# A two-layer streaming encoder step: the main product stream of layer 0 shifted against its chain, and three small changes of order beside it

## The chip, the cores and the metric

The kernel runs on one core of one Trainium2 chip, as one program. The time is the device time of one execution in microseconds (us); the value of a kernel is the median of its runs. The profile is that of a single execution, recorded by the hardware profiler. The core's engines are TensorE (matmul, PE in the profile, with its weight loads as PEld), VectorE (DVE), ScalarE (ACT), GpSimd (POOL), and SyncE (SP), whose queue here issues nearly all DMAs.

## What is computed

The reference is one inference step of two layers over 512 prompt tokens and 32 sample tokens, width 1024. Layer 0 mixes tokens with RWKV-7, layer 1 with differential attention; both also attend to 256 memory rows in 4 heads and gate the result. Only layer 0 is touched by the change:

```python
def rwkv_layer(x, mk, mv, prev_row, S0, norm_w, w_out, w_in, mu, ...):
    h = rmsnorm(x, norm_w)
    p, qm, gate = jnp.split(h @ w_in, [RW_PROJ, RW_PROJ + MEM_W], axis=-1)
    y_mix, S_T, last_row = rwkv_mixer(p, prev_row, S0, mu, w0, w_up, a0, a_up, k_k, k_a, r_k, ln_w, ln_b)
    y_mem = mem_attention(qm, mk, mv)
    out = jnp.concatenate([y_mix.astype(x.dtype), y_mem], axis=-1) * jax.nn.silu(gate)
    return x + out @ w_out, S_T, last_row

# in rwkv_mixer, for each of 24 heads, token by token (S is 64 x 64):
def step(S, inp):
    r_t, k_t, v_t, w_t, kk_t, a_t = inp
    sa = jnp.einsum('bhvk,bhk->bhv', S, -kk_t)
    S = (S * w_t[:, :, None, :] + sa[..., None] * (kk_t * a_t)[:, :, None, :]
         + v_t[..., None] * k_t[:, :, None, :])
    return S, jnp.einsum('bhvk,bhk->bhv', S, r_t)

# mem_attention, per head: softmax(q k^T / sqrt(128)) v over 256 memory rows
```

The sample tokens start from a state that is given (`state_rwkv`), the prompt from zero.

## The kernel before

**Heads, pairs, chunks.** The 24 heads are worked in 12 pairs (two heads of 64 fill the 128 partitions). Within a pair the 512 prompt tokens are 8 chunks of 64, and the state goes from chunk to chunk: this is the *chain* (`rw_chain`, `chunk`). A chunk takes three steps. TensorE multiplies the state `SB` with the prepared operand `zr`, and VectorE adds the result into `avz`; TensorE multiplies `avz` with `at`, and ScalarE copies the result into `sv` and `yt` and scales the old state into `sd`; TensorE multiplies `sv` with `bt`, and VectorE makes the new state from it. The first chunk lacks the first step, so a pair has 23 chain steps. Each begins with a TensorE instruction that must wait for VectorE or ScalarE.

**The main stream.** The large projection `h @ w_in` (and the memory values) is cut into blocks of 128 output columns. A block is 48 matmuls of 128x272, here called main products: two token halves, eight slices of the inner dimension, and three products each, since every fp32 operand is split into a high and a low part (`whi`, `wlo` of the weights, `hh`, `hl` of the activations). `stream` (L1535) is a generator that gives the products of all blocks one at a time, so that they can be laid between the chain steps; in the trace they write the tile `ps_g`. At the head of a block it asks for weights two blocks ahead (`load`, two DMAs of 256 KB on SP's queue into `raw`) and puts the split of the next block's weights (ScalarE makes `whi`, VectorE `wlo`) on a list. At the end of a half block the result is evacuated: for a shift block, ScalarE copies it to `raw`, and a scaling (ScalarE) and an addition (VectorE, the tile is called `rkv`) are put on the same list; for a gate block, a tanh and a multiplication (`sg`).

**The put-off list.** `some` (L313) is called once per half step. It takes at most one VectorE item and one ScalarE item off the head of the list, a VectorE item only if an allowance permits. The allowance is `room` times the half steps so far, less what VectorE has been given already (`spent`), by the estimates in the plan. `until` empties the list up to an item when a reader needs it.

**The plan.** Each engine executes its instructions in the order in which the program issues them, and that order is written out by hand here. `PLAN` (L48) has one entry for each of the 23 steps of a pair, with two halves. Each names pieces of other work: `prep` prepares a later pair, `inv`, `back`, `at` and `mrg` invert small triangular blocks on GpSimd by way of DRAM, `val`, `out` and `fin` finish outputs, `smp` is the sample's chunk (`rw_sample`), `rsq` a reciprocal root. The two numbers beside a piece are its estimated time on TensorE and on VectorE. In pairs 10 and 11 there is nothing left to prepare, and `MPLAN` (L77) lays the steps of the memory attention there (`mem_steps`, L1223), one entry per call: keys and values are fetched, then per group of two token tiles the scores, the softmax, the transposes and at last the product with the values. `scores` has VectorE take the row maximum (`mnm`), and ScalarE the exponentials (`mp`, with their row sums `mrs`), and `weighted` has VectorE scale them. The PSUM pool of most of these small products, `psm`, has two buffers (L2160).

**How many products per step.** `each[pr]` is the number of main products of a pair: 192 in most pairs (four blocks), 144 in pair 9, which has only three, and 130 left over in pair 0. In pair 9, `KEPT` = 24 of them stay behind for the end of the pair. `whole` sums the TensorE estimates of the pair and 0.126 us per product, `due` cuts it into 23 equal parts (in pair 0 by the estimated VectorE load), and each half step issues products until its due time is reached. The blocks in their order are: for pair p up to 8, the k block of pair p+3, the gate of pair p-1, the r block and the v block of pair p+3; then queries, gates, and the first blocks of the output projection.

**The sample's state.** `rw_sample` (L983) fetches the pair's given state by two DMAs into `SS`, at its first call (step 4), transposes it there (`ps_si`), and goes through the chunk at the later `smp` entries.

Of the kernel before, what the change touches and what calls it, by code (L numbers as in the profile page):

```python
# [45 lines left out]
LATER = 0.75  # L46
FULL = ("full", 0, 0, 0)
PLAN = [  # L48
    [[("val", 0, 0.95, 0), ("prep", 2, 0.1, 0)], [("prep", 2, 0, 0.42)]],
    [[], [("prep", 2, 0, 1.04)]],  # L50
# [21 lines left out]
MEMPE = 4.8  # L72
SHIFTED, KEPT = 13, 24
LAM = 5
EARLY = 5
SPLIT = {10: (18,), 11: (1, 5, 9, 13)}
MPLAN = {10: [(0, 0), (2, 0), (3, 0), (4, 0), (5, 0), (6, 0), (6.5, 1), (7, 0), (8, 0), (9, 0), (10, 0), (11, 0), (11.5, 0), (12.5, 1),  # L77
# [3 lines left out]

# [26 lines left out]
class Trunk:  # L108
# [874 lines left out]
    def rw_sample(self, st):  # L983

        nc, p, pr = self.nc, self.rb2, st["pr"]
        sl = self.SS[pr % 2]
        for h in range(2):
            self.se.dma_start(sl[64 * h : 64 * h + 64, 64 * h : 64 * h + 64], self.a["state_rwkv"][0, 0, 2 * pr + h])
        yield
        ps = self.psm.tile([P, 4, P], F32, tag="m", name="ps_si")  # L990
        self.te.transpose(ps[:, 0, :], sl[:], self.ident[:])
        S = p.tile([P, P], F32, tag="ssi", name="ssi", bufs=1)
        self.ve.tensor_copy(S[:], ps[:, 0, :])
        yield from self.chunk(st, 8, S, sl)
        yield
        self.state_out(sl, self.o[8][0, 0, 2 * pr : 2 * pr + 2])
# [226 lines left out]
    def mem_steps(self, st, i, h, p, two):  # L1223
# [25 lines left out]
        def scores(tiles):  # L1249
# [9 lines left out]
            pt = p.tile([P, 2, NMEM], F32, tag="mp", name="mp", bufs=2)  # L1259
            self.ve.tensor_reduce(nm[:, :k], s, AX.X, ALU.max, negate=True)  # L1260
            for u in range(k):
                self.ae.activation(pt[:, u, :], s[:, u], AF.Exp, bias=nm[:, u : u + 1], accum_out=rs[:, u : u + 1])
# [18 lines left out]
        for t in groups[:2]:  # L1281
            yield
            scores(t)
            yield
            weighted()
# [5 lines left out]
        yield  # L1291
        scores(groups[2])
        yield
# [132 lines left out]
    def layer0(self, mem):  # L1426
# [6 lines left out]
        with ExitStack() as ctx:  # L1433
# [160 lines left out]
            for kind, n in zip(("mrg", "mrg", "val", "mrg"), FILL3):  # L1594
                go(kind, 0)
                fill(n)
            ready = len(FILL2) - 11
            each[0] -= sum(map(sum, (FILL0, FILL1, FILL2, FILL3))) - 4 * 24 - 6 * 48
            for pr in range(NPAIR):
# [3 lines left out]
                load = [HOPV[k % 3] + sum(us for x in y for kind, d, _, us in x if 0 <= pr + d < NPAIR) for k, y in enumerate(PLAN)]  # L1603
                whole = sum(took) + MEMPE * len(mplan) / 12 + MAIN * (each[pr] - kept)

                pace = [max(x, 1.4) for x in load] if each[pr] < 3 * 6 * KT else [1.0] * len(PLAN)
                due = [whole * sum(pace[:k]) / sum(pace) for k in range(len(PLAN) + 1)]
                room = (sum(load) + 2.3 * each[pr] / 48) / len(PLAN)
                t, left, spent = 0.0, each[pr] - kept, 0.0
                for k, y in enumerate(PLAN):  # L1610
# [3 lines left out]
                    for half, x in enumerate(y):  # L1614
# [7 lines left out]
                        for at, h in mplan:  # L1622
                            if at == k + half / 2:
                                if h not in mit:
                                    mit[h] = self.mem_steps(mems[h], 0, h, self.ma, 2)
                                    next(mit[h])
                                next(mit[h], None)
                                t += MEMPE / 12
                        if half and pr == LAM and k in (1, 7):
# [599 lines left out]
```

## Time and profile before

| | |
|---|---|
| runs | 1404.84 us median of 3 (1404.56 to 1409.58) |
| profiled execution | 1403.86 us, its span 1401.7 us |
| mean granted TensorE clock | 0.996 |
| layer 0, pairs 0 to 11 | 134.97 to 692.00 us of the span |
| HBM read and written | 111.12 MB and 22.91 MB |

The page's first part gives the busy time of each engine; its second part shows the span in 40 slices, where TensorE stands at 9 tenths or more in all slices but the first and the last. A matmul's end is modelled and reaches into the next one, so short pauses of TensorE do not show as idle time. The page's share of a line is of little use here, because one helper (L105) records every operation; the names of tiles tell the places apart. In the views, `a<-b,c` is a tile and what it was made from, and `[1.39 <-DVE avz]` is the idle time before an instruction and what ended it. In the lists of waits the three numbers are the total in us, the count, and the longest.

### The profile page before, as it was taken

To read this page: it belongs to the slowest core of one execution; us is meant where nothing else is said; L and a number is where in the kernel's file an instruction comes from. 1 tells how busy PE (TensorE), PEld (TensorE's weight loads), DVE (VectorE), ACT (ScalarE), POOL (GpSimd) and SP (SyncE) were. 2 spreads that over 40 slices of the span, in tenths; PEclk is the share of its full clock that TensorE was granted. 3 is DMA by queue.
4 is the path that set the end of the run, shared out by engine and by line. 5 is a ranking of instruction groups with operands and counts; after the bars stand their busy time and mean duration, and the time that the engine had idled before them with its cause. 6 is when DMAs were issued, how large, how long until landed. Compare 5 with 4: busy or idle time off the path is not lost.

```text
span 1401.7 us, 31899 instructions
## 1 busy us (share of the span) xinstructions
PE 1366.8 (98%) x11881; PEld 1304.5 (93%) x11881; DVE 932.2 (67%) x2345; ACT 825.4 (59%) x2292; POOL 376.2 (27%) x840
## 2 busy tenths in 40 slices
PE   8999999999999999999999999999999999999997
PEld 6998899999999998898899999999999999999997
DVE  5676777787877787666753476666467756767443
ACT  5765677767776777565543366664466546665222
POOL 2136568555865586520000040000000001001100
PEclk9999999999999999999999999999999999999999
DMA  7543222332233223342364474333333322332321
GB/s 224 155 119 83 61 54 64 84 86 71 69 81 97 61 64 82 81 136 71 114 201 125 124 211 114 92 91 87 107 92 92 104 75 84 94 107 86 91 76 72
DMA packets 264036, 139.45 MB, mean 99 GB/s; under 512 B 57721, under 2 KB 252802, under 8 KB 263882
## 3 DMA queue, kind: packets, MB, share of 16 engines
q1 hardware_dynamic: 263818, 137.41, 34.9%
q8 instruction: 94, 1.54, 0.5%
q14 instruction: 60, 0.49, 0.1%
q10 hardware_dynamic: 64, 0.02, 0.0%
HBM read 111.12 MB, written 22.91 MB: 96 GB/s over the span
## 4 chain that ended last, share of the span: by engine, by line
PE 83%; DVE 8%; ACT 4%; DMA 2%; issue 2%; SPq 1%; DVEq 0%; ACTq 0%
PE ps_g L105 58%; PE ps_c L105 5%; PE ps_s L105 2%; PE ps_o L105 2%; PE ps_at L105 2%; DVE wlo L105 2%; PE ps_v L105 1%; PE ps_mo L105 1%; SPq L105 1%; PE ps_mm L105 1%; PE ps_aT L105 1%; PE ps_w L105 1%; PE ps_yc L105 1%; PE ps_ss L105 1%; PE ps_kv L105 1%
## 5 line engine op out<-in xcount | busy, mean ns | idle before, releaser
L105 PE MATMUL ps_g<-hh,wlo 128*128 128x272 f32 x1808 | 537.8, 298 | 2.4 <-DVE wlo L105 2.4
L105 PE MATMUL ps_g<-hh,whi 128*128 128x272 f32 x1808 | 538.3, 298 | 0.4 <-DVE memk L105 0.2
L105 PE MATMUL ps_g<-hl,whi 128*128 128x272 f32 x1808 | 531.9, 295 | 0.6 <-DVE hl L105 0.3
L105 PEld LDWEIGHTS ps_g<-hh,wlo 128*128 128x128 f32 x1808 | 340.9, 189 | 7.9 <-DVE wlo L105 3.5
L105 PEld LDWEIGHTS ps_g<-hh,whi 128*128 128x128 f32 x1808 | 341.7, 189 | 5.1 <-DVE og L105 0.6
L105 PEld LDWEIGHTS ps_g<-hl,whi 128*128 128x128 f32 x1808 | 341.4, 189 | 4.6 <-DVE hl L105 1.2
L105 DVE TENSOR_TENSOR wlo<-raw,whi 128x512 fp32r<-128x512 f32 x314 | 220.0, 712 | 116.8 <-ACT whi L105 112.9
L105 ACT CAST whi<-raw 128x512 fp32r<-128x512 f32 x314 | 188.8, 618 | 108.4 <-PE ps_g L105 61.3
L853 POOL TENSOR_TENSOR tm<-u,m 102x84 f32<-102x84 f32 (+23 forms) x341 | 147.9, 434 | 165.5 <-DMA m<-sc 139.7
L855 POOL TENSOR_TENSOR u<-u,tm 102x84 f32<-102x84 f32 (+23 forms) x341 | 148.9, 437 | 26.7
L105 PE MATMUL ps_g<-hi,whi 128*128 128x272 f32 x512 | 148.9, 291 | 0.0
L105 PE MATMUL ps_g<-hi,wlo 128*128 128x272 f32 x512 | 147.7, 288 | 0.5 <-DVE wlo L105 0.5
L105 PE MATMUL ps_g<-lo,whi 128*128 128x272 f32 x512 | 147.4, 288 | 0.0
L1325 POOL TENSOR_TENSOR lo<-og,hi 128x544 fp32r<-128x544 f32 x8 | 13.2, 1652 | 359.5 <-ACT hi L105 359.1
L105 PEld LDWEIGHTS ps_g<-hi,wlo 128*128 128x128 f32 x512 | 96.4, 188 | 0.7 <-DVE wlo L105 0.7
L105 PEld LDWEIGHTS ps_g<-hi,whi 128*128 128x128 f32 x512 | 96.5, 188 | 0.0
L105 PEld LDWEIGHTS ps_g<-lo,whi 128*128 128x128 f32 x512 | 96.5, 188 | 0.0
L105 DVE SCALAR_TENSOR_TENSOR SB<-ps_c,dl,sd 64x64 f32<-64x64 f32 x168 | 47.5, 283 | 43.6 <-PE ps_c L105 37.2
L105 ACT ACTIVATE pt<-ps_s,snm 128x128 f32<-128x128 f32 (+3 forms) x96 | 50.9, 531 | 41.7 <-DVE snm L105 41.6
L1746 POOL TENSOR_TENSOR hl<-hn,hh 128x544 fp32r<-128x544 f32 x8 | 12.4, 1564 | 209.8 <-ACT hh L105 209.7
L105 ACT COPY sv<-ps_c 64x64 f32<-64x64 f32 x192 | 39.3, 205 | 44.3 <-PE ps_c L105 42.6
L105 ACT ACTIVATE sg<-ps_g 128x272 f32<-128x272 f32 x64 | 25.3, 395 | 56.1 <-PE ps_g L105 51.6
(399 smaller groups left out, 2586.8 us busy)
## 6 DMA issues: line engine op xcount, KB each, us to landing
raw<-in_rw_in_dram SPq DMA_DIRECT2D x114, 256.0 KB
raw<-in_df_in_dram SPq DMA_DIRECT2D x112, 256.0 KB
raw<-in_w_out_dram SPq DMA_DIRECT2D x64, 256.0 KB
oscr<-sg SPq DMA_DIRECT2D x16, 272.0 KB
lo<-oscr SPq DMA_DIRECT2D x16, 272.0 KB
m<-sc SPq DMA_DIRECT2D x33, 128.0 KB
raw<-in_w_mem_v_dram SPq DMA_DIRECT2D x16, 256.0 KB
kh<-kh SPq DMA_DIRECT2D x24, 136.0 KB
```

What stands on the lines that cost most here:

```text
L105: return lambda *a, **k: self.trunk.tie(self, issue(*a, **k))
L853: nc.gpsimd.tensor_tensor(tm[:, :n, :wd], u3[:, :n, kx : kx + 1].to_broadcast(sh), m3[:, kx : kx + 1, kx + 1 :].to_broadcast(sh), ALU.mult)
L855: nc.gpsimd.tensor_tensor(u3[:, :n, kx + 1 :], u3[:, :n, kx + 1 :], tm[:, :n, :wd], ALU.add)
L1325: (self.nc.gpsimd if g % 2 and self.o1 else self.ve).tensor_tensor(lo[:], t, hi[:].bitcast(F32), ALU.subtract)
L1746: nc.gpsimd.tensor_tensor(self.hl[:, k, :], h[:], self.hh[:, k, :].bitcast(F32), ALU.subtract)
```

## The change

Four things are changed, all in layer 0, and the work itself stays the same.

- `LAG` = 4: each of pairs 0 to 8 issues four main products fewer between its chain steps, and pair 9 issues the 36 that are then outstanding. The stream's order is unchanged; it runs behind the chain by four more products with each pair, and is level again at the end of pair 9.
- In `mem_steps`, layer 0 alone, the exponentials become a step of their own behind the maximum. `MPLAN` gets three more entries per head, in most places half a step behind the scores, and the estimate of 4.8 us per head is spread over 15 steps instead of 12.
- The allowance `room` of pairs 10 and 11 takes in the splits of gated tiles (`SPLIT`) at 0.75 us each: one in pair 10, four in pair 11.
- `smp` gets an entry at step 0, at which the sample's state is asked for; the transpose stays at step 4.

```diff
--- before.py
+++ after.py
@@ -46,7 +46,7 @@
 LATER = 0.75
 FULL = ("full", 0, 0, 0)
 PLAN = [
-    [[("val", 0, 0.95, 0), ("prep", 2, 0.1, 0)], [("prep", 2, 0, 0.42)]],
+    [[("val", 0, 0.95, 0), ("prep", 2, 0.1, 0), ("smp", 0, 0, 0)], [("prep", 2, 0, 0.42)]],
     [[], [("prep", 2, 0, 1.04)]],
     [[("prep", 1, 0.53, 0)], [("prep", 1, 0, 0), ("prep", 2, 0.56, 1.0)]],
     [[("prep", 2, 0, 0)], [("prep", 2, 0, 1.0)]],
@@ -70,14 +70,16 @@
     [[("prep", 3, 0, 1.45), ("val", 1, 0.45, 0)], [("prep", 3, 0, 0.5)]],
     [[("out", 0, 1.6, 0.7)], [("prep", 3, 0, 0)]]]
 MEMPE = 4.8
-SHIFTED, KEPT = 13, 24
+SHIFTED, KEPT, LAG = 13, 24, 4
 LAM = 5
 EARLY = 5
 SPLIT = {10: (18,), 11: (1, 5, 9, 13)}
-MPLAN = {10: [(0, 0), (2, 0), (3, 0), (4, 0), (5, 0), (6, 0), (6.5, 1), (7, 0), (8, 0), (9, 0), (10, 0), (11, 0), (11.5, 0), (12.5, 1),
-              (14, 1), (15, 1), (16, 1), (17, 1), (18, 1), (19, 1), (19.5, 1), (19.5, 2), (20, 1), (21, 1), (22, 1)],
-         11: [(1.5, 2), (2, 2), (3, 2), (4, 2), (4.5, 3), (5, 2), (6, 2), (7, 2), (7.5, 2), (8, 2), (9, 2), (10, 3), (11, 2),
-              (11, 3), (12, 3), (13, 3), (14, 3), (15, 3), (16, 3), (17, 3), (18, 3), (19, 3)]}
+MPLAN = {10: [(0, 0), (2, 0), (3, 0), (3.5, 0), (4, 0), (5, 0), (5.5, 0), (6, 0), (6.5, 1), (7, 0), (8, 0), (8.5, 0), (9, 0),
+              (10, 0), (11, 0), (11.5, 0), (12.5, 1), (14, 1), (14.5, 1), (15, 1), (16, 1), (16.5, 1), (17, 1), (18, 1), (19, 1),
+              (19.5, 1), (19.5, 2), (20, 1), (20.5, 1), (21, 1), (22, 1)],
+         11: [(1.5, 2), (2, 2), (2.5, 2), (3, 2), (4, 2), (4.5, 2), (4.5, 3), (5, 2), (6, 2), (7, 2), (7.5, 2), (8, 2), (8.5, 2),
+              (9, 2), (10, 3), (11, 2), (11, 3), (11.5, 3), (12, 3), (13, 3), (13.5, 3), (14, 3), (15, 3), (16, 3), (16.5, 3),
+              (17, 3), (18, 3), (19, 3)]}
 
 FILL0 = [4, 4, 8, 2, 6, 2, 2, 2, 6, 2, 18, 4, 4, 2, 2, 0, 8, 12, 4, 8, 14, 10, 6, 14, 2, 0, 2, 2, 2, 2, 2, 2]
 FILL1 = [6, 14, 12, 2, 4, 2, 2, 2, 8, 0, 10, 0, 2, 8, 8, 6, 4, 6, 6, 8, 18, 12, 8, 10, 0, 0, 0, 0, 4]
@@ -984,6 +986,7 @@
 
         nc, p, pr = self.nc, self.rb2, st["pr"]
         sl = self.SS[pr % 2]
+        yield
         for h in range(2):
             self.se.dma_start(sl[64 * h : 64 * h + 64, 64 * h : 64 * h + 64], self.a["state_rwkv"][0, 0, 2 * pr + h])
         yield
@@ -1258,6 +1261,8 @@
             rs = p.tile([P, 2], F32, tag="mrs", name="mrs", bufs=2)
             pt = p.tile([P, 2, NMEM], F32, tag="mp", name="mp", bufs=2)
             self.ve.tensor_reduce(nm[:, :k], s, AX.X, ALU.max, negate=True)
+            if two > 1:
+                yield
             for u in range(k):
                 self.ae.activation(pt[:, u, :], s[:, u], AF.Exp, bias=nm[:, u : u + 1], accum_out=rs[:, u : u + 1])
             made.append((tiles, pt, rs))
@@ -1280,7 +1285,7 @@
 
         for t in groups[:2]:
             yield
-            scores(t)
+            yield from scores(t)
             yield
             weighted()
         yield
@@ -1289,7 +1294,7 @@
         pT = p.tile([P, 2, T], F32, tag="mpT", name="mpT")
         turned(*made[0])
         yield
-        scores(groups[2])
+        yield from scores(groups[2])
         yield
         weighted()
         yield
@@ -1595,17 +1600,20 @@
                 go(kind, 0)
                 fill(n)
             ready = len(FILL2) - 11
+            for pr in range(9):
+                each[pr] -= LAG
+            each[9] += 9 * LAG
             each[0] -= sum(map(sum, (FILL0, FILL1, FILL2, FILL3))) - 4 * 24 - 6 * 48
             for pr in range(NPAIR):
                 mplan = MPLAN.get(pr, ())
                 kept = KEPT if pr + 3 == NPAIR else 0
                 took = [HOP + sum(us for x in y for kind, d, us, _ in x if 0 <= pr + d < NPAIR) for y in PLAN]
                 load = [HOPV[k % 3] + sum(us for x in y for kind, d, _, us in x if 0 <= pr + d < NPAIR) for k, y in enumerate(PLAN)]
-                whole = sum(took) + MEMPE * len(mplan) / 12 + MAIN * (each[pr] - kept)
+                whole = sum(took) + MEMPE * len(mplan) / 15 + MAIN * (each[pr] - kept)
 
                 pace = [max(x, 1.4) for x in load] if each[pr] < 3 * 6 * KT else [1.0] * len(PLAN)
                 due = [whole * sum(pace[:k]) / sum(pace) for k in range(len(PLAN) + 1)]
-                room = (sum(load) + 2.3 * each[pr] / 48) / len(PLAN)
+                room = (sum(load) + 2.3 * each[pr] / 48 + LATER * len(SPLIT.get(pr, ()))) / len(PLAN)
                 t, left, spent = 0.0, each[pr] - kept, 0.0
                 for k, y in enumerate(PLAN):
                     go("chain", pr)
@@ -1625,7 +1633,7 @@
                                     mit[h] = self.mem_steps(mems[h], 0, h, self.ma, 2)
                                     next(mit[h])
                                 next(mit[h], None)
-                                t += MEMPE / 12
+                                t += MEMPE / 15
                         if half and pr == LAM and k in (1, 7):
                             (self.lam_in if k == 1 else self.lam_out)()
                         if half and pr == NPAIR - 2 and k == SHIFTED:
```

## The prediction, made before the change was run

> **What bounds the kernel now.** The page comes first: it says whether any engine has room at all.
>
> ```profile
> span 1401.7 us, 31899 instructions
> PE 1366.8 (98%) x11881; PEld 1304.5 (93%) x11881; DVE 932.2 (67%) x2345; ACT 825.4 (59%) x2292; POOL 376.2 (27%) x840
> ```
>
> TensorE is busy 98% of the span, and the change adds and removes no product. So only TensorE's idle time can be won, 34.9 us in all (1401.7 - 1366.8). The question is how much of it lies where the change works. I cut layer 0's main loop at the first chain product of each pair (the first `ps_c<-avz,at` of a pair in the timeline) and asked for busy time in these stretches. Each row has the stretch, its length, the busy time (and instructions) of TensorE, its weight loads, VectorE, ScalarE and GpSimd, then TensorE's granted clock, the DMA share and GB/s; here pairs 8, 9, 10 and 11.
>
> ```profile
> 501.48:547.44 45.96, 45.65 (x468) 42.95 (x468) 36.01 (x91) 33.21 (x96) 29.42 (x65) 1.00 0.28 73
> 547.44:591.63 44.19, 39.23 (x409) 35.88 (x409) 32.25 (x81) 26.87 (x81) 27.76 (x69) 1.00 0.22 55
> 591.63:641.57 49.94, 48.65 (x452) 44.34 (x450) 32.40 (x83) 29.65 (x95) 12.92 (x36) 1.00 0.43 123
> 641.57:692.00 50.43, 47.05 (x379) 42.61 (x379) 34.08 (x86) 29.80 (x93) 0.00 (x0) 1.00 0.25 75
> ```
>
> Pair 8 is full: 0.31 us idle. Pair 9 idles 4.96 us, pair 10 1.29, pair 11 3.38. The same cut for the main products alone (tile `ps_g`) says why, for pairs 8 and 9:
>
> ```profile
> 501.48:547.44 45.96, 30.33 (x193) 25.62 (x192) 0.85 (x2) 3.12 (x8) 1.00 0.28 73
> 547.44:591.63 44.19, 24.26 (x145) 19.59 (x144) 1.27 (x3) 2.34 (x6) 1.00 0.22 55
> ```
>
> By the weight loads pair 8 has 192 main products to lay between its 23 chain steps, pair 9 only 144. In the waits, TensorE in pair 9 waited for:
>
> ```profile
> PE ps_c L105 <- DVE avz L105: 1.4, 1, 1.4
> PE ps_w L105 <- DVE t1b L105: 1.3, 2, 1.1
> PE ps_c L105 <- DVE SB L105: 1.0, 2, 0.5
> PE ps_at L105 <- DVE bk L105: 0.9, 1, 0.9
> PE ps_c L105 <- ACT yt L105: 0.3, 1, 0.3
> ```
>
> Nearly all of it is VectorE coming late, though VectorE is busy only 32.25 of 44.19 us there. Its timeline at the pair's start shows a backlog, and TensorE's row beside it the longest wait:
>
> ```profile
> 551.30 0.78 DVE L105 SCALAR_TENSOR_TENSOR rkv<-raw,PA,rkv 128x544 f32<-128x544 f32 x1 [1.18 <-ACT raw L105]
> ...
> 553.16 0.28 DVE L105 TENSOR_TENSOR avz<-ps_c,avz 64x128 f32<-64x128 f32 x1
> 553.36 0.67 DVE L105 TENSOR_TENSOR wlo<-raw,whi 128x512 fp32r<-128x512 f32 x1
> ...
> 560.59 0.90 DVE L105 TENSOR_TENSOR bk<-rkv,cum 128x512 f32<-128x512 f32 x2
> ```
> ```profile
> 553.49 0.49 PE L105 MATMUL ps_c<-avz,at 128*128 128x128 f32 x2 [1.39 <-DVE avz L105]
> ```
>
> The put-off add of the third shift block (`rkv`) waits for ScalarE, and the 0.28 us addition that the chain needs stands behind it. That is the reading on which the rest stands: pair 9 lacks products as cover, its neighbours have enough. Pair 0 is a case of its own. Three stretches of its 43 us (134.97 to 178.15) show TensorE first idling 1.13 us, then at a lower granted clock (0.76, 0.50, 0.74):
>
> ```profile
> 164.00:167.40 3.40, 2.27 (x31) 1.94 (x32) 2.17 (x6) 0.83 (x2) 0.00 (x0) 0.76 0.51 137
> 167.40:170.80 3.40, 3.40 (x34) 3.34 (x30) 1.28 (x8) 1.60 (x6) 1.45 (x7) 0.50 0.64 181
> 170.80:174.20 3.40, 3.40 (x23) 3.25 (x24) 0.95 (x5) 1.77 (x6) 2.69 (x10) 0.74 0.43 118
> ```
>
> **The change part by part.** *Products later.* One main product costs 9.02/72 = 0.125 us:
>
> ```profile
> 723.24 9.02 PE ps_g L105 x72
> ```
>
> Four later is 0.50 us less work in each of pairs 0 to 8, and 36 x 0.125 = 4.51 us more in pair 9. Without new waits the full pairs give back 8 x 0.50 = 4.00 us. That they can is shown by TensorE's waits over all of pairs 1 to 8:
>
> ```profile
> PE ps_w L105 <- DVE bv L105: 0.8, 4, 0.2
> PE ps_y L105 <- DVE yt L105: 0.8, 3, 0.3
> ```
>
> These two are nearly all of it, 1.6 us in eight pairs; cover is lost at four of some 46 half steps in each. New waiting lies between 0 and all 4.00 us; I take 0.4, near the end that 1.6 us in 8 x 46 half steps points to. Pair 0 idles already, 1.13 us in the first of its stretches above, so its 0.50 us mostly turns into idling: 0.2 won. The products also bring evacuations, weight splits and shift adds up to 36 products (some 4.4 steps) later against the chain; the allowance, which lets one out only when VectorE has spent less than the average so far, hides that. Where it fails, one wait like the 1.39 us above comes with it.
>
> In pair 9 the loop lays 156 instead of 120 products over 23 steps (24 stay behind for its end): 1.57 more each, 0.196 us of cover per step. Seven waits shrink by that at least: 1.4 us, the lower bound (zero if one 1.39 us wait takes their place). The upper bound is 4.96. Between them: VectorE works from 551.30 to 561.49 without a pause, six steps in which 1.39 + 0.5 + 0.9 us of waiting fall. These get 6 x 0.196 = 1.18 us of cover, and lose the 0.78 us add and the two splits of 0.67 us of that block boundary, which move five steps on (36/6.8): 3.3 us against 2.8, all gone. The later waits, 2.2 us, lose 0.196 in each of four, 0.8, and the moved VectorE work costs some 0.2 where it now falls. Sum: 3.4 us won, of which I trust the first half most.
>
> Against 4.51 more and 4.20 less work, the balance is 4.51 - 3.4 - 4.00 - 0.2 + 0.4 = -2.7 us.
>
> *Exponentials as own step, allowance, prices.* In pairs 10 and 11 the longest waits of ScalarE and of TensorE, and one of VectorE's, are:
>
> ```profile
> ACT mp L105 <- DVE mnm L105: 18.1, 10, 4.8
> ```
> ```profile
> PE ps_c L105 <- ACT yt L105: 1.5, 4, 0.6
> PE ps_g L105 <- DVE wlo L105: 0.8, 1, 0.8
> ```
> ```profile
> DVE mrs L105 <- ACT mp L105: 1.1, 4, 0.6
> ```
>
> ScalarE stands 18.1 us at the head of its queue with exponentials whose maximum VectorE hasn't made. One such place, ScalarE's timeline and TensorE's row:
>
> ```profile
> 647.73 0.47 ACT L105 ACTIVATE mp<-ps_mm,mnm 128x256 f32<-128x256 f32 x1 [2.00 <-DVE mnm L105]
> ...
> 648.64 0.62 ACT L105 CAST whi<-raw 128x512 fp32r<-128x512 f32 x1
> ...
> 649.44 0.42 ACT L105 COPY sv<-ps_c 64x64 f32<-64x64 f32 x2
> ```
> ```profile
> 650.18 0.49 PE L105 MATMUL ps_c<-sv,bt 128*128 128x128 f32 x2 [0.55 <-ACT yt L105]
> ```
>
> With the exponentials half a step later, the cast (0.62) goes into the 2.00 us pause, and `sv` is no longer late. But the chain's copy still stands behind the exponentials, so only what is put off between them is won. And the softmax's reciprocal on VectorE stays one step after the maximum: where it waits already (`mrs`, 1.1 us) it may wait up to half a step longer, with the chain's additions queued behind it and TensorE waiting for those. Of the 1.5 us I take 0.9, less 0.2 for that: 0.7 (bounds 1.5 won, and as much again of `mrs`, 1.1, lost). The allowance grows by 0.75/23 = 0.03 us per step in pair 10 and 4 x 0.75/23 = 0.13 in pair 11, 3 us by its end, so the weight split on which the stretch after the loop waited (0.8) comes earlier: 0.5 (0 to 0.8). Sum 1.2 us. The same 4.8 us spread over 15 steps instead of 12 moves a product here or there; nothing is added.
>
> *Sample state.* Its DMA is issued and its first reader runs at, in pair 9:
>
> ```profile
> 545.64 1.11 SPq L105 DMA_DIRECT2D SS<-in_state_rwkv_dram  x2
> ```
> ```profile
> 555.17 0.27 PE L105 MATMUL ps_si<-ident,SS 128*128 128x128 f32 x1
> ```
>
> That is 8 us between issue and use, with no wait in front of the reader. Asking sooner wins nothing; it guards against weight loads that now hold the same queue longer. What it is moved past on SP slips by at most 1.1 us, and no TensorE wait quoted here is for a DMA; POOL's queue is not passed.
>
> **Sum.** -2.7 - 1.2 = -3.9 us. The profiled execution took 1403.86 us (span 1401.7), the median of the runs is 1404.84, 0.98 above. So 1399.96 on the profile's footing, and 1401.0 as a median.
>
> **The rivals.** *More room than idle time shows* (12%). A matmul's recorded end reaches into the next one, so short waits can hide inside busy time. Weight loads of pair 8 fill 42.95/45.96 = 93.4% of it; at that share pair 9's 35.88 us need 38.4, so 5.8 could be won, and pair 11's 42.61 us need 45.6, so 4.8. With 5.8 and half of the 4.8 the sum is 4.51 - 5.8 - 4.20 + 0.4 - 2.4 = -7.5: 1397.3. Against it: most of pair 9's waits are dependencies that stay. [...]
>
> *The backlog only moves* (20%). The block boundary lands on the next heavy steps of pair 9, and one 1.39 us wait returns there: 1.4 won, less 1.39; with pairs 10 and 11 giving half: 4.51 - 0 - 4.20 + 0.4 - 0.6 = +0.1: 1404.9.
>
> *Pair 0's clock* (6%, either way). Its granted clock falls in and after the stretch in which TensorE was busy 2.27 of 3.40 us. The three rows make some 6.8 us at half speed ((0.24 + 0.50 + 0.26) x 3.4 / 0.5), which cost 3.4. With four products fewer, a second such stretch may follow (1404.4), or the first may fall elsewhere and not trip (1397.6). The stretch is quiet with or without these products, so I expect it to stay. [...]
>
> *PSUM held longer, slower* (7%). The scores' buffer is one of two (`psm`), and it is freed by the exponentials. Already now a transpose waits for that:
>
> ```profile
> 634.30 0.66 PE L105 MATMUL ps_mt<-ident,mp 128*128 128x128 f32 x4 [0.63 <-ACT mp L105]
> ```
>
> Half a step later is 49.94/46 = 1.09 us later. It decides where two other `psm` tiles are asked for between maximum and exponentials. At six of the twelve groups that costs 6.5 us: 1404.84 - 2.7 + 6.5 = 1408.6; at all twelve 13.0, 1415.1. For it: the row above. Against: in pairs 10 and 11 no preparation competes for these buffers.
>
> **Chances.** The forecast has 55%, its own range is 1398.5 to 1403.0. The range, from 1396.0 (most of the hidden room) to 1405.5 (backlog back), leaves out the PSUM case and the edge of the first rival. About 0.5% (7.0 us) is what a measurement of this kernel can tell from no change: faster means below 1397.8, which needs more than half of the first rival, the lucky half of the clock, and a tail of the forecast: 0.16. Slower means above 1411.9, half of the PSUM case: 0.04. The rest is 0.80.
>
> **What would show it.** Right, if pairs 1 to 8 take some 0.5 us less each (45.5), pair 9 about 45.3 with 180 products and under 2 us of idle time, pairs 10 and 11 together 1.2 us less, the wait of `mp` for `mnm` well under 18.1 us, and the state's reader still without a wait. Wrong, if pairs 1 to 8 keep their 46 us with new waits for `avz` or `SB`, if pair 9 grows by the full 4.5 us, if `ps_mt` or `ps_mm` wait more for `mp`, or if the half-speed stretch of pair 0 is gone or doubled.

## The result, and the profile after

The change made the kernel slower: 1413.99 us median of 8 runs (1410.14 to 1416.93) against 1405.99 (1404.56 to 1409.58) for the kernel before beside it, a ratio of 1.0058 with a 95% interval of 1.0046 to 1.0070. That is +8.0 us where -3.9 was forecast. The profiled execution is the slowest of the eight, 1416.93 us, and the one profiled before, 1403.86 us, is a little under its fastest run, so sums over their rows come to +13.1 us and not to +8.0.

The page's first lines, after:

```profile
span 1414.8 us, 31939 instructions
PE 1374.7 (97%) x11881; PEld 1314.8 (93%) x11881; DVE 934.4 (66%) x2345; ACT 823.7 (58%) x2292; POOL 366.0 (26%) x840
```

TensorE is recorded 7.9 us longer busy with the same 11881 instructions, and idle for 40.1 us instead of 34.9. Both have to be explained. The same cut by pairs, here pairs 0, 3, 6, 8, 9, 10 and 11 (length; busy time of TensorE, its weight loads, VectorE, ScalarE, GpSimd; granted clock, DMA share, GB/s):

```profile
135.81:180.16 44.35, 41.30 (x394) 37.85 (x393) 28.25 (x73) 27.68 (x81) 27.05 (x71) 0.90 0.26 64
...
272.21:319.20 46.99, 45.06 (x464) 42.46 (x464) 36.55 (x91) 32.51 (x96) 27.78 (x62) 1.00 0.30 75
...
415.36:463.54 48.18, 46.51 (x464) 43.92 (x464) 35.93 (x91) 32.74 (x96) 27.70 (x63) 0.96 0.28 74
...
513.44:562.84 49.40, 46.53 (x464) 43.98 (x464) 36.87 (x90) 32.59 (x95) 23.99 (x60) 0.97 0.26 67
562.84:607.04 44.20, 43.02 (x445) 40.29 (x445) 33.48 (x83) 28.73 (x84) 28.06 (x65) 1.00 0.26 65
607.04:657.20 50.16, 48.40 (x451) 44.17 (x450) 32.50 (x83) 29.66 (x95) 10.27 (x30) 1.00 0.43 121
657.20:707.50 50.30, 48.68 (x394) 44.43 (x394) 35.47 (x89) 30.11 (x93) 0.00 (x0) 1.00 0.28 82
```

Pair 8 took 45.96 us before and takes 49.40. Two columns tell it apart from the old row: idle time (length less TensorE's busy time) is 2.87 us instead of 0.31, and the granted clock is 0.97 instead of 1.00. Pair 9 is the opposite: its length is unchanged, its idle time fell from 4.96 to 1.18 us. The main products alone, pairs 8 and 9:

```profile
513.44:562.84 49.40, 31.03 (x189) 26.21 (x188) 0.87 (x2) 3.10 (x8) 0.97 0.26 67
562.84:607.04 44.20, 28.95 (x181) 24.03 (x180) 1.29 (x3) 2.71 (x7) 1.00 0.26 65
```

So 36 products moved as announced: 188 by weight loads in pair 8, 180 in pair 9. Stretch by stretch the 13.1 us of the profiled execution are: ahead of pair 0 +0.8, pair 0 +1.2, pairs 1 to 8 +13.4 (382.68 after, 369.29 before), pair 9 0.0, pairs 10 and 11 +0.1, all that follows -2.4.

**The new waits.** TensorE's two longest waits over pairs 3 to 8 of the kernel after (total, count, longest):

```profile
PE ps_at L107 <- DVE bk L107: 7.2, 6, 2.1
PE ps_w L107 <- DVE t1b L107: 1.6, 4, 0.6
```

`ps_at` is part of the preparation of a later pair: products of `zr` with `bk`, two groups of 16 per pair at fixed steps, of which the first (step 7) waits. Before, it waited for nothing in these pairs. `ps_w` holds the 32x32 products that merge the inverted triangular blocks (`mrg`), with VectorE's transposition `t1b` as operand. VectorE's timeline of the kernel before, in pair 6 up to the `bk` in question:

```profile
413.20 0.82 DVE L105 SCALAR_TENSOR_TENSOR rkv<-raw,PA,rkv 128x544 f32<-128x544 f32 x1 [0.67 <-ACT raw L105]
...
421.21 0.93 DVE L105 TENSOR_TENSOR bk<-ba,cum 128x512 f32<-128x512 f32 x2
...
422.50 0.92 DVE L105 TENSOR_TENSOR bk<-rkv,cum 128x512 f32<-128x512 f32 x2
423.34 0.77 DVE L105 SCALAR_TENSOR_TENSOR rkv<-raw,PA,rkv 128x544 f32<-128x544 f32 x1
```

The add of one block (the first row) is done 7 us ahead of the first `bk`, the add of the next (the last row) stands behind the last `bk`, and `ps_at` starts at 423.62, straight after a chain product. The same place after:

```profile
425.58 0.78 DVE L107 SCALAR_TENSOR_TENSOR rkv<-raw,PA,rkv 128x544 f32<-128x544 f32 x1 [0.34 <-ACT raw L107]
...
426.72 0.73 DVE L107 TENSOR_TENSOR ba<-nk,na 128x544 f32<-128x544 f32 x1
427.36 0.76 DVE L107 TENSOR_TENSOR wlo<-raw,whi 128x512 fp32r<-128x512 f32 x1
428.05 0.88 DVE L107 TENSOR_TENSOR bk<-ba,cum 128x512 f32<-128x512 f32 x2
...
429.28 0.88 DVE L107 TENSOR_TENSOR bk<-rkv,cum 128x512 f32<-128x512 f32 x2
```
```profile
430.19 1.05 PE L107 MATMUL ps_at<-zr,bk 64*128 64x128 f32 x14 [1.04 <-DVE bk L107]
```

When this pair starts, 24 products have slid, three steps' worth. With them the first of the two block ends came later against the chain: in the kernel before its add stood 3.9 us into the pair (413.20 from 409.33), now it stands 10.2 us into it (425.58 from 415.36). So its put-off work, the add (0.78 us) and a split (`wlo`, 0.76), is now in VectorE's queue right ahead of `bk`. TensorE waits 1.04 us.

**The clock.** Two stretches of the kernel after with the one ahead of each:

```profile
400.63:404.04 3.41, 3.34 (x52) 2.91 (x51) 2.34 (x8) 0.47 (x4) 2.67 (x10) 1.00 0.12 30
404.04:407.45 3.41, 3.41 (x16) 3.41 (x17) 1.93 (x8) 2.15 (x8) 2.86 (x8) 0.50 0.50 145
448.41:451.82 3.41, 2.80 (x39) 2.48 (x40) 1.91 (x7) 1.27 (x4) 2.60 (x10) 1.00 0.41 117
451.82:455.24 3.42, 3.42 (x36) 3.35 (x30) 2.38 (x9) 1.45 (x6) 2.82 (x8) 0.50 0.42 111
```

In the second and the fourth row the clock is granted at 0.50; such a fall to half speed is called a trip below. Six such stretches lie in the layer up to pair 8: 3.41 us each from 356.25, 404.04, 451.82 and 530.33, and 6.83 us from 168.52 and from 499.61; one more of 3.41 lies ahead of pair 0, at 134.38. Before there was one, 6.83 us in pair 0. Ahead of five of the six stands the quiet part of a pair, steps 15 to 17, in which TensorE has many tiny products:

```profile
449.04 1.28 PE L107 MATMUL ps_ss<-hsel,sq 128*128 128x2 f32 x10 [0.55 <-ACT bt L107]
...
451.20 1.17 PE L107 MATMUL ps_w<-t1b,at 32*32 32x32 f32 x32
```

The sixth, from 530.33, stands elsewhere: ahead of it lies the 2.1 us wait of `ps_at` in pair 8.

```profile
526.92:530.33 3.41, 1.31 (x19) 1.14 (x18) 2.90 (x8) 0.11 (x1) 0.00 (x0) 1.00 0.15 42
```

For pairs 1 to 8 the terms are then: products -4.0; idle time +9.2 (12.7 us, 382.68 less 370.01, after; 3.5, 369.29 less 365.81, before); half speed up to +10.2 (20.5 us at half). That makes 15.4 where 13.4 was measured. Half speed costs less where TensorE would have waited anyway; that this is the difference is likely and not shown.

### The profile page after: what moved, and what is told of

It reads as the page before. It is cut to its first block, busy times and chain, and to the rows that moved or that the text cites. A ratio compares the mean times of both kernels' runs of the same rounds, so it can differ in the third digit from the quotient of the medians.

```text
span 1414.8 us, 31939 instructions
## 1 busy us (share of the span) xinstructions
PE 1374.7 (97%) x11881; PEld 1314.8 (93%) x11881; DVE 934.4 (66%) x2345; ACT 823.7 (58%) x2292; POOL 366.0 (26%) x840
## 4 chain that ended last, share of the span: by engine, by line
PE 81%; DVE 8%; ACT 6%; issue 2%; DMA 2%; SPq 1%; POOL 0%; DVEq 0%; POOLq 0%; ACTq 0%
PE ps_g L107 56%; PE ps_c L107 4%; PE ps_s L107 2%; PE ps_at L107 2%; PE ps_o L107 2%; PE ps_v L107 2%; DVE wlo L107 2%; PE ps_mo L107 1%; ACT sv L107 1%; PE ps_w L107 1%; PE ps_mm L107 1%; SPq L107 1%; PE ps_aT L107 1%; PE ps_wa L107 1%; PE ps_yc L107 1%
## 5 line engine op out<-in xcount | busy, mean ns | idle before, releaser
L107 PEld LDWEIGHTS ps_g<-hl,whi 128*128 128x128 f32 x1808 | 345.1, 191 | 4.6 <-DVE hl L107 1.3
L857 POOL TENSOR_TENSOR u<-u,tm 102x84 f32<-102x84 f32 (+23 forms) x341 | 135.7, 398 | 26.7
```

What stands on the lines that cost most here:

```text
L107: return lambda *a, **k: self.trunk.tie(self, issue(*a, **k))
L857: nc.gpsimd.tensor_tensor(u3[:, :n, kx + 1 :], u3[:, :n, kx + 1 :], tm[:, :n, :wd], ALU.add)
```

## The experiments

Two theories stand against each other at first, and a third for the clock. **Theory A:** the place decides. Each pair's lag adds up, the block ends slide against the steps, and their put-off work comes ahead of what the chain or the preparation needs. **Its rival:** the count decides. Four products fewer leave a full pair without enough cover, wherever the block ends lie. (In the expectations the place is A or A1, the count A2 or C; in the first two experiments B stands for the other three parts of the change. The clock's gate is there whatever it is that lowers the granted clock.) **The clock:** it is either a by-product of the waits or a cause with a price of its own. All edits below are to the kernel named; the medians of the kernel before, which ran beside each group, are 1404.5 to 1405.1 us.

**The lag alone.** The kernel before with the one part:

```diff
+            for pr in range(9):
+                each[pr] -= 4
+            each[9] += 9 * 4
```

> The kernel before with the lag alone (four products later per pair, 36 more in pair 9). Theory A, the lag moves block-end work onto the steps ahead of ps_at: TensorE waits for bk of some 1 us or more return in each of pairs 3 to 8, 6 to 8 us in all, some half-speed stretches of the clock among them, and the time is 1409 to 1416 us. Theory B, the slower time comes from the exponentials, the allowance or the sample state: no such waits, pairs 1 to 8 at 45.6 us, 1400 to 1404 us.

Measured: 1414.81 us (1411.14 to 1420.14), ratio 1.0073 (1.0048 to 1.0098). The whole loss is this part. TensorE's first wait over pairs 3 to 8:

```profile
PE ps_at L105 <- DVE bk L105: 6.2, 6, 1.2
```

One in every pair, as in the kernel after, without any of the other three parts.

**All but the lag.** The kernel after with `LAG` = 0.

> The changed kernel with a lag of 0, so the exponentials, the allowance and the sample state alone. Theory A: pairs 1 to 9 as in the kernel before (46.1 and 44.2 us), pairs 10 and 11 within 1 us of before, 1403 to 1406 us. Theory B: new waits in pairs 10 and 11 or at the state's reader, over 1409 us.

Measured: 1402.29 us (1400.93 to 1403.57), ratio 0.9984 (0.9974 to 0.9993), about 2.2 us won, a little better than either expectation. So the lag costs 1.0058/0.9984, 0.74% or 10.4 us.

**Sliding without fewer products.** The kernel before; pair 1 gives 24 products to pair 9, and pairs 2 to 8 have their 192 again, but every block end in them lies 24 products later:

```diff
+            each[1] -= 24
+            each[9] += 24
```

> The kernel before with 24 products taken from pair 1 and given to pair 9; pairs 2 to 8 keep 192 products each, but their block ends stand 24 products later against the chain. Theory A1, the place of the block ends decides: a wait of ps_at for bk of about 1 us in each of pairs 2 to 8, 7 us in all, less some 3 us that pair 9 gives back, 1406 to 1413 us. Theory A2, the number of products as cover decides: pairs 2 to 8 at 46.1 us without new waits, only pair 1 waits, 1401 to 1404 us.

Measured: 1408.75 us (1408.16 to 1414.17), ratio 1.0036 (1.0022 to 1.0050). The wait for `bk` over pairs 2 to 8, and two pairs (pair 6 and pair 9):

```profile
PE ps_at L105 <- DVE bk L105: 7.1, 7, 1.2
```
```profile
412.12:458.40 46.28, 45.31 (x468) 42.98 (x468) 36.13 (x91) 32.74 (x96) 26.77 (x60) 1.00 0.31 80
...
551.57:595.52 43.95, 41.36 (x434) 38.73 (x434) 32.61 (x82) 27.82 (x83) 26.51 (x63) 1.00 0.24 58
```

Seven pairs, seven waits for `bk`, with all products in place: pair 6 has its 468 instructions and idles 0.97 us instead of 0.47 (46.17 us long, 45.70 busy before). The place of the block ends suffices for the wait. Two half-speed stretches of 3.41 us came too, in pairs 3 and 4 (from 305.62 and 353.40; the granted clock is 0.96 in both pairs). Pair 9 lays 24 products more in 43.95 us, less than its 44.19 before, so the winning half of the change works here too.

**Fewer products without sliding.** The kernel before; each gate block of pairs 1 to 8 leaves out its four `hl` products of slices 2 and 5, and the pair issues four less:

```diff
                 for t, x in ((0, self.hh), (0, self.hl), (1, self.hh)):
+                    if short and k in (2, 5) and x is self.hl:
+                        continue
...
+            for pr in range(1, 9):
+                each[pr] -= 4
```

> The kernel before, but four products of each gate block in pairs 1 to 8 are left out (the low part of the activations in two of eight slices), so these pairs have 188 products as in the changed kernel, while the block ends keep their place at the pairs' ends. Theory A1: 0.5 us less per pair, no new waits, 1400 to 1402 us. Theory A2: the waits of the changed kernel appear in pairs 3 to 8, 1407 us or more.

Measured: 1415.33 us (1412.45 to 1415.94), ratio 1.0070 (1.0055 to 1.0085), slower although 32 products are missing, and outside what the place alone let expect (1400 to 1402). The wait for `bk` is gone, but another is there, over pairs 2 to 8:

```profile
PE ps_w L105 <- DVE t1b L105: 5.9, 14, 0.7
```

In VectorE's timeline the transposition `t1b` stands ahead of the put-off add in the kernel before, and behind it here:

```profile
258.63 0.90 DVE L105 STREAM_TRANSPOSE t1b<-at 32x256 f32<-32x256 f32 x2
259.47 0.73 DVE L105 SCALAR_TENSOR_TENSOR rkv<-raw,PA,rkv 128x544 f32<-128x544 f32 x1
```
```profile
261.51 0.79 DVE L105 SCALAR_TENSOR_TENSOR rkv<-raw,PA,rkv 128x544 f32<-128x544 f32 x1
262.33 0.90 DVE L105 STREAM_TRANSPOSE t1b<-at 32x256 f32<-32x256 f32 x2
```

With the gate block shorter, the block ends behind it come earlier against the steps, so this kernel moved block ends after all and is no clean trial of the count. It says two things none the less: two items that change places in VectorE's queue cost 0.4 us of TensorE, twice per pair; and the clock tripped here without any lag: it is granted at 0.93 in pair 1 and at 0.96 in pairs 3 to 6, and four of the half-speed stretches start 47.78 us apart, as in the kernel after.

**The put-off work held back.** The kernel after; the list is not served in steps 3 to 6 of pairs 1 to 8:

```diff
-                        if FULL not in x:
+                        if FULL not in x and not (1 <= pr <= 8 and 3 <= k <= 6):
```

> The changed kernel, but in steps 3 to 6 of pairs 1 to 8 nothing is taken off the put-off list, so no put-off add or split stands before the making of bk on VectorE unless a reader forces it. Theory A (put-off work ahead of bk makes ps_at wait): the waits of ps_at for bk fall from 7 us to under 2 us over pairs 3 to 8, and the time by 3 to 6 us, to 1408 to 1411 us, less if the put-off work makes another product wait. Theory C (the chain itself is too short of cover with 188 products): these waits stay.

Measured: 1420.72 us (1419.25 to 1425.44), ratio 1.0124 (1.0102 to 1.0145). TensorE's waits over pairs 3 to 7, the two longest:

```profile
PE ps_g L107 <- ACT whi L107: 5.7, 5, 1.4
PE ps_g L107 <- DVE wlo L107: 3.1, 4, 1.1
```

The wait for `bk` has gone from these pairs and from pair 8, which shows its cause (one of 1.5 us is left in pairs 1 and 2). The time is 9 us and more above the 1408 to 1411 that were expected. In its place the main products wait for their own weight split, 8.8 us in five pairs. The slid block end has no cheap place: its split cannot wait for these four steps either.

**Half the lag.** The kernel after with `LAG` = 2.

> The changed kernel with a lag of 2 instead of 4. Theory A: what decides is how far the block ends have slid, so pairs 1 to 5 (up to 12 products) wait as little as pairs 1 and 2 of the changed kernel, and pairs 6 to 8 as much as its pairs 3 and 4, 1 us or more each; 1404 to 1409 us. Theory C (products as cover): half of the changed kernel's waits in every pair.

Measured: 1405.01 us (1403.49 to 1407.61), ratio 1.0004 (0.9995 to 1.0014). The waits for `bk`, first over pairs 3 to 5 and then over pairs 6 to 8:

```profile
PE ps_at L107 <- DVE bk L107: 1.0, 3, 0.4
...
PE ps_at L107 <- DVE bk L107: 2.8, 3, 1.0
```

The wait grows with the distance slid: 6 to 10 products at the start of the first three pairs, 12 to 16 at that of the last three. (In the kernel after it doesn't grow evenly: 1.2, 1.2, 0.6, 1.0, 1.0 and 2.1 us in pairs 3 to 8.)

**Cover for pair 9 from the other side.** The kernel after with `LAG` = 0; pair 9 takes 20 products from pairs 10 and 11, so that no block end ahead of it moves:

```diff
+            each[9] += 20
+            each[10] -= 10
+            each[11] -= 10
```

> The changed kernel with a lag of 0, and 20 products given to pair 9 from behind instead of from before: 10 each from pairs 10 and 11, which then come sooner. Theory A: pairs 1 to 8 keep their 46.1 us, pair 9 loses some 2.5 us of idle time and grows by nothing, pairs 10 and 11 shrink by 1 us each or wait as much more; 1399 to 1402 us. Theory C: the waits go to pairs 10 and 11, 1402 to 1405 us.

Measured: 1402.92 us (1401.69 to 1406.29), ratio 0.9994 (0.9985 to 1.0003), nothing on top of the kernel without lag. Pairs 9 and 10:

```profile
547.20:593.56 46.36, 42.26 (x429) 38.41 (x429) 33.74 (x84) 28.13 (x84) 29.93 (x75) 1.00 0.28 71
593.56:644.12 50.56, 47.43 (x441) 42.98 (x440) 32.48 (x83) 29.65 (x95) 10.39 (x29) 1.00 0.42 121
```

Pair 9 still idles 4.1 us, and pair 10, which idled 1.29 us in the kernel before and 1.70 in the kernel without lag, now idles 3.1. The cover was only moved.

**More products in the quiet part.** The kernel after, lag and all; steps 15 and 16 of pairs 1 to 8 get a larger share of their pair's products:

```diff
+                if 0 < pr < 9:
+                    pace[15] = pace[16] = 1.4
```

> The changed kernel with the same products per pair, but in pairs 1 to 8 steps 15 and 16, in which the small ps_ss and ps_w products run, get 40% more time and so some three more main products each, and the other steps correspondingly fewer. If the clock's gate trips because TensorE does too little in that stretch, the half-speed stretches in pairs 1 to 8 go (mean clock 0.995 or more, 1409 to 1411 us). If the gate answers to the 1 to 2 us waits of ps_at at step 7, or to chance alone, they stay as they are (0.990 to 0.993, 1413 to 1417 us).

Measured: 1405.77 us (1404.10 to 1407.29), ratio 1.0006 (0.9996 to 1.0015). Pair 6, and the waits for `bk` over pairs 3 to 8:

```profile
413.20:459.39 46.19, 44.95 (x466) 42.59 (x462) 36.09 (x90) 32.05 (x95) 27.41 (x60) 1.00 0.29 76
```
```profile
PE ps_at L107 <- DVE bk L107: 8.0, 6, 1.8
```

The waits are all there, but pair 6 is back at 1.00 and takes 46.19 us instead of 48.18. One 3.41 us stretch at half speed is left in pairs 1 to 8, and it lies behind the wait of `ps_at` in pair 5 (from 381.57; 0.97 over that pair), not behind a quiet part. Pairs 1 to 8 idle 12.9 us as against 12.7, and take 374.69 us instead of 382.68. So the clock is a cause with its own price.

How large that price is stays open within bounds. Of the lag's 0.74%, 0.52% (1.0058 less 1.0006, 7.3 us) went with this edit, more than the 3 to 5 us that were expected, and not all of it is the clock: pair 9 takes 43.18 us instead of 44.20, at 1.00 in both. One run of the kernel after had a mean clock of 0.996 and still took 1410.14 us, 4.2 more than the kernel before; and the profiled execution of the lag alone took 1413.57 us with one half-speed stretch of 6.83 us in pairs 1 to 8. An estimate from the mean clocks of the runs (0.9916 over the eight of the kernel after, 0.9952 over the ten here) is 0.0036 of 1412 us, 5.1 us. So some 4 to 7 of the lag's 10.4 us are the clock's, and the other 3 to 6 are waiting that pair 9 does not pay for.

**The same tilt without the lag.** The edit above, on the kernel after with `LAG` = 0.

> The changed kernel with a lag of 0 and the same 40% more time for steps 15 and 16 in pairs 1 to 8. If the tilt helped the changed kernel by way of the clock alone, there is little to win here, since without the lag only one stretch of pairs 1 to 8 or none was at half speed: 1401 to 1403 us, as without the tilt. If it helped by better cover of the waits, pairs 1 to 8 get shorter than 46 us: under 1400 us.

Measured: 1401.90 us (1400.90 to 1403.35), ratio 0.9979 (0.9969 to 0.9988). The interval overlaps that of the kernel without lag (0.9974 to 0.9993): not told apart. Pairs 1 to 8 take 370.1 us in both profiled executions, so the better cover that was to bring them under 46 us each did not show.

**The tilt in pair 0 too, and in pair 9 ahead.** Again with `LAG` = 0:

```diff
+                if pr < 9:
+                    pace[15], pace[16] = 1.4 * pace[15], 1.4 * pace[16]
+                if pr == 9:
+                    pace[:7] = [1.3] * 7
```

> As the run before, with the tilt in pair 0 too, and 30% more time for the first seven steps of pair 9, where VectorE is behind. If pair 0's half-speed stretch comes from the same place, it goes or is halved (1.7 to 3.4 us); pair 9 loses 1 to 2 us of its 4.7 us of idle time, or the waits of its later steps grow by as much. 1397 to 1401 us; no gain over the run before if pair 0's stretch stays and pair 9's waits move.

Measured: 1401.03 us (1399.83 to 1403.19), ratio 0.9974 (0.9965 to 0.9983). This is the lowest median of all versions, below both kernels; but its interval overlaps those of the two other versions without lag, the one before and the plain one, so which of its parts does anything is not settled. Pair 0's stretch stayed at 6.83 us (from 166.99); pair 9 idles 3.4 us instead of 4.7, with one stretch of 3.41 us at half speed in it.

**Fewer products in the quiet part.** The kernel before, without lag or any other part:

```diff
+                if 0 < pr < 9:
+                    pace[15] = pace[16] = 0.6
```

> The kernel before, but steps 15 and 16 of pairs 1 to 8 get 40% less time and so some three products fewer each; products per pair and block ends stay. If the clock's gate trips on that stretch, half-speed stretches appear in pairs 1 to 8 without any lag (mean clock 0.988 to 0.993) and the time is 1408 to 1416 us. If the lag is needed for them, the clock stays at 0.995 to 0.996 and only small waits come: 1404 to 1407 us.

Measured: 1443.71 us (1443.16 to 1446.08), ratio 1.0284 (1.0267 to 1.0301). One full pair, and the half-speed stretches of two:

```profile
329.88:381.13 51.25, 48.08 (x468) 45.33 (x468) 37.25 (x91) 33.42 (x95) 25.10 (x60) 0.93 0.26 68
```
```profile
366.19:373.02 6.83, 5.49 (x50) 5.30 (x51) 5.59 (x15) 2.94 (x9) 5.76 (x14) 0.50 0.08 19
417.39:424.22 6.83, 5.82 (x52) 5.62 (x53) 5.28 (x15) 2.77 (x9) 5.81 (x14) 0.50 0.07 19
```

The same products in the same pairs, spread a little otherwise: +39 us, 4.9 per pair, far above the 1408 to 1416 us that were expected. In the pair shown (pair 4) 2.7 us more are idle (51.25 less 48.08 is 3.17, against 0.46 before), and the clock takes up to 3.4, half of 6.83. This is no trial of the clock alone: over pairs 2 to 8 TensorE waits 9.8 us for `t1b`, 5.7 for `bk` and 3.8 for `bt`, so the edit shifted the block ends against the steps as well. It does show half-speed stretches without any lag, with the clock at 0.93 in pairs 3 to 6.

**The exponentials and the state without the allowance.** The kernel after with `LAG` = 0 and the old `room`:

```diff
-                room = (sum(load) + 2.3 * each[pr] / 48 + LATER * len(SPLIT.get(pr, ()))) / len(PLAN)
+                room = (sum(load) + 2.3 * each[pr] / 48) / len(PLAN)
```

> The changed kernel with a lag of 0 and the allowance as before: the exponentials as own step and the sample state alone. Without the lag, the other three parts together won 2.4 us. By the prediction's terms the exponentials hold 0.7 of 1.2 and the allowance 0.5, so some 1.4 us should be left, 1402.9 to 1403.9 us, with the wait for the weight split at the end of pair 11 (0.8 us) back. If the exponentials hold all of it, the time stays at 1402.3; if the allowance does, it is 1404.5 or more.

Measured: 1403.46 us (1402.16 to 1405.52), ratio 0.9990 (0.9981 to 0.9999). In pairs 10 and 11 TensorE's wait for the weight split is back:

```profile
PE ps_g L107 <- DVE wlo L107: 0.9, 1, 0.9
```

So exponentials and state together win about 1.4 us, and the allowance about another 0.8 (the two intervals overlap; the wait that it takes away, 0.9, agrees).

## Why the prediction was wrong, point by point

**The step that failed** is the new waiting under *Products later*: "New waiting lies between 0 and all 4.00 us; I take 0.4". In the profiled execution pairs 1 to 8 have 9.2 us more idle time, more than twice the upper bound. The bound supposed that a pair with four products fewer can lose at most the cover of those four. But the slide adds up, and the waits come from where the block ends fall, not from the count: with 192 products in each pair they came all the same (the sliding alone, 7.1 us in seven pairs). The prediction had the slide in sight ("up to 36 products (some 4.4 steps) later against the chain") and let the allowance hide it. The allowance limits how much VectorE work is let out up to a step; it doesn't know what the work is put in front of. The sign that was named for this, waits for `avz` or `SB`, had the wrong tile too: the waits were for `bk`. The one price given for its failure, "one wait like the 1.39 us above", was about the right size (1.2 us in the mean over pairs 3 to 8, 2.1 at most), but it comes in each pair from pair 3 on and not once.

**The clock** was weighed for pair 0 alone. It costs some 4 to 7 us of the lag's 10.4, in pairs that showed 1.00 before, and pair 0's own stretch stayed, as forecast. That the other pairs could come to it as well could not be read from their busy time: a quiet part of the kernel before that did not trip was recorded just as busy as one of the kernel after that did (3.35 and 3.34 of 3.41 us, below). What differs between these two is the main products in them, 11 and 6.

**Pair 9** went as described: 180 products in the old length, idle time 4.96 to 1.18. The forecast had 3.4 us won for 4.5 us of work; 4.5 were won in 44.20 against 44.19 us. Of these 3.8 are idle time, and the remaining 0.7 were hidden inside recorded busy time: the first rival's mechanism is there, at a small size. It could not outweigh the rest.

**Pairs 10 and 11** were forecast 1.2 us shorter. Their idle time fell by 1.3 (1.29 + 3.38 before, 1.76 + 1.62 after), but they did not get shorter: TensorE does 15 instructions more in pair 11, and what follows is 2.4 us shorter. The three parts by themselves won 2.2 us (the kernel without lag) where 1.2 was forecast, so this term had the right sign and was too small. The longest waits of TensorE's chain and of ScalarE there, after:

```profile
PE ps_c L107 <- ACT yt L107: 1.0, 3, 0.4
```
```profile
ACT mp L107 <- DVE mnm L107: 17.0, 11, 4.8
```

The wait for `yt` fell from 1.5 to 1.0, the one for `wlo` (0.8) is gone. What was named as the mark of this step, "well under 18.1 us", did not show: ScalarE still stands 17.0 us in front of its exponentials. So half a step was mostly not enough for the maximum to be made. What goes ahead of the exponentials now may be what was won; that is argued, not shown.

**The sample's state** is asked for earlier, and its reader waits for nothing, as before. In pair 8, the issue and the first reader:

```profile
509.67 1.78 SPq L107 DMA_DIRECT2D SS<-in_state_rwkv_dram  x2
```
```profile
521.39 0.27 PE L107 MATMUL ps_si<-ident,SS 128*128 128x128 f32 x1
```

**The rivals.** The backlog that "only moves" in pair 9 did not come; it moved in pairs 3 to 8 instead. No wait on PSUM took its place. The slower end was given 4%, and to the wrong mechanism.

**What stays open.** What the clock goes by isn't shown; the columns counted below differ between two cases, but do not decide all. Nor is the clock's share of the lag's price, beyond 4 to 7 us. That half-speed stretches explain the spread of the runs is argued: the mean clocks and the times of the runs go together (1410.14 us at 0.996, 1416.93 at 0.988), but not strictly. The count of products by itself was not tried cleanly, since leaving any out moves a block end.

## What to carry to other kernels

Where one stream is shifted against a hand-ordered chain, a small shift per round adds up: ask for the total distance which queue items it carries past which, and price each crossing once per round, not once. Spare work belongs in the round that lacks cover only if the ends of blocks in the other rounds stay where they were; undoing that one part while keeping the rest gave 0.9984 where the whole gave 1.0058. Look at the granted clock of each round in an experiment's profile before blaming waits, and give the quiet part of a round products from its full part: two numbers in a list took the kernel after from a ratio of 1.0058 to 1.0006, some 7 us. Without the lag the same two numbers won nothing that could be told apart (0.9979 with them, 0.9984 without), so here this paid only where stretches at half speed showed.

## What the runs showed of the hardware

**The half-speed stretches start whole multiples of 3.41 us apart, and a loop may lock to that.** In the kernel after, the seven starts listed above lie 10, 55, 14, 14, 14 and 9 times 3.413 us apart; those of pairs 4 to 6 are 47.79 and 47.78 us apart, 14 times 3.413. Those of the slowest experiment start 51.20 us apart (366.19 to 417.39), 15 times 3.413. The lengths inside the layer are one or two times 3.41 us (3.41 and 6.83). Such distances don't show a lock yet. What speaks for one is the length of the pairs: in the slowest experiment pairs 3 to 6 take 51.36, 51.25, 51.03 and 51.20 us, with a stretch in each, so that the quiet part of the next pair falls on the same place, counted in steps of 3.413 us, and trips again. In the kernel after it is only nearly so: a full pair without a trip takes 46.0 to 47.0 us, one trip lengthens it to about 48 (48.18, 47.98 and 48.18 in pairs 4 to 6), and the stretch creeps from 37.05 us into pair 4 to 36.46 into pair 6. The times are measured; the lock is the reading that fits them.

**The same recorded busy time stood ahead of half speed and of full speed.** Here are two stretches of 3.41 us with the quiet part of a pair in them: from the kernel after, with a half-speed stretch behind it (404.04), and from the kernel before (pair 6, 81 times 3.413 us behind the start of its stretch in pair 0, 165.74), with none. The first row of each has all instructions, the second the main products alone (without the column of GpSimd):

```profile
400.63:404.04 3.41, 3.34 (x52) 2.91 (x51) 2.34 (x8) 0.47 (x4) 2.67 (x10) 1.00 0.12 30
400.63:404.04 3.41, 1.03 (x6) 0.84 (x7) 0.00 (x0) 0.00 (x0) 1.00 0.12 30
...
442.22:445.63 3.41, 3.35 (x52) 3.08 (x52) 2.67 (x9) 2.43 (x7) 2.78 (x9) 1.00 0.17 44
442.22:445.63 3.41, 1.74 (x11) 1.48 (x11) 0.00 (x0) 0.15 (x1) 1.00 0.17 44
```

Both have 52 products and the same busy time, but 6 main products against 11. So they differ in the columns of their matmuls (by the shapes in the timeline 272 in a main product, 128 in one of the chain, 32 or 2 in the tiny ones): by the products that start in them, the first has some 2900 columns and the second some 4400. The count does not decide every case. The 3.41 us ahead of the seven half-speed stretches of the kernel after have 1156 to 3474 columns; a stretch of the same kernel with 2772 (from 305.05), and two of the kernel before with 3172 and 3316 (from 210.11 and 302.27, in pairs 1 and 3), had full speed behind them.

Nor did it take a long wait: in the kernel after the longest wait ahead of a trip in pairs 1 to 8 is 2.1 us (pair 8), and of the 3.41 us ahead of 404.04 TensorE is recorded busy for all but 0.07.
